# Issuing a kernel's side stream of weights from GpSimd's queue, and spacing its first part wider

## The chip, the cores and the metric

The kernel runs on one core of a Trainium2 chip. The metric is the device time of one execution in microseconds. Before the change three runs took 2155.38, 2155.86 and 2158.86 us, median 2155.86.

## The reference

One block of a network on 256 tokens of 2048 numbers, all in float32: a feed-forward layer, a mixer and a second feed-forward layer, each wrapped in the same way.

```python
def sandwich_sublayer(x, fn, gain_pre, gain_post, shift, scale, gate, weight):
    h = modulate(rms_norm(x, gain_pre), shift, scale)
...
def swiglu(h, w_gate, w_up, w_down):
    return (jax.nn.silu(h @ w_gate) * (h @ w_up)) @ w_down
...
    return jnp.concatenate([y_pool, y_rwkv], axis=-1) @ w_out
```

Each sublayer adds its gated, normalized result to `x`. The feed-forward layers have 5632 hidden numbers; the mixer projects with `w_in`, runs a pooling branch and a recurrence (24 heads of 64), and projects back with `w_out`. The nine vectors of the **modulation** (shift, scale and gate of three sublayers) are one product of a single row, `silu(c) @ w_ada + b_ada`, with a weight matrix of 2048 x 18432: 151 MB, used for nothing else. Vectors 0 to 2 belong to the first feed-forward layer (FFN1), 3 to 5 to the mixer, 6 to 8 to the second (FFN2).

## The kernel before

**Products.** Every weight tile is split in two parts for the sake of precision: ACT copies it to a rounded `hi` (L179), DVE subtracts to get `lo` (L180), and PE makes three products of each tile (`mm3` L189 to L191, `mm3_wide` L196 and L197, `rows_mm` L523 to L525). I call such a pair of hi and lo a piece. Pieces have four buffers, so DVE and ACT can be at most four pieces ahead of PE. The weights themselves come by `load` (L169), one DMA of up to 1 MB on SyncE's queue (SP), into four raw buffers in the FFNs and two in the mixer.

**The modulation** runs beside all this on DVE. `ada_begin` (L205) lists its work as 76 steps in the order of vectors (1,0), 2, 4, 3, 5, 7, 6, 8. The first 20 steps make vectors 1 and 0 together, ahead of FFN1's first products, with transfers of 256 KB (L238). Each later vector has eight steps, four for either half: a step (`ada_step`, L220) issues four transfers of 512 KB on SP (L235) into tiles named `ada` (four buffers in the FFNs, two in the mixer), and DVE multiplies each by its part of silu(c) and adds it to an accumulator, `acc` (L242 for the first, L244 for the others). After the last of a half vector DVE transposes the accumulator (L256), reduces it (L258), PE makes four small products (L261), and DVE adds the bias into `mod` (L264). These DVE instructions are given low priority (`later`), and a scheduler that works on the whole program sets the order in which they stand on DVE between the splits. Every engine then runs its own list in that order.

**When a step is begun.** The layers call `tick` at each chunk of weights, and every so many chunks it begins a step: `ADA_FFN1` = 2.8 in FFN1 (L616, 84 chunks tick), 3 in the mixer (42 chunks tick) and in its last product w_out (16), 12 in FFN2. At fixed places `ada_finish` (L267) begins all the steps that are still missing for a vector: vector 3 before FFN1's last product, vector 5 before w_out, vector 6 before w_out's last quarter (L847, `q == 3`), vector 8 before FFN2's last product. In FFN1 84 / 2.8 gives 30 steps: the 24 of vectors 2, 4 and 3, and six of vector 5.

**FFN1** goes through gate and up for the first hidden columns with all of the reduction (`outer`), its down product, then two more groups of gate, up and down. Its pieces are number 0 to 263 in DVE's order; those of the mixer 264 to 504, with w_out from 441 on, in the quarters q = 0 (two at once), 2 and 3; FFN2's follow.

**The last quarter of w_out** is written by `rows_block` with `apart`: it has three banks, `sb` (first 128 tokens), `y` and `mm` (two halves of the others), and the pieces of its last eight rows are held back, so that each bank is finished apart. `mm` stands in a pool of two banks that the modulation's small products (L261) share.

Of the kernel before, what the change touches and what calls it, by code (L numbers as in the profile page):

```python
# [18 lines left out]
D = 2048  # L19
# [8 lines left out]
TICKS = (1, 3, 7)  # L28
GROUPS1 = (20, 16, 8)
GROUPS2 = (12, 12, 12, 8)  # L30
ADA_FFN1, ADA_MIXER, ADA_OUT, ADA_FFN2 = 2.8, 3, 3, 12
BLOCKS = ((0, 2), (2, 2), (4, 4), (8, 4), (12, 4))
POOL_WIDTH = 512
POOL_WINDOWS = (2, 4, 8, 16)
# [42 lines left out]
class Block:  # L77
# [142 lines left out]
    def ada_step(self, psum):  # L220
        nc = self.nc
        if self.ada_pos == len(self.ada_tasks):
            return
        cols, k0 = self.ada_tasks[self.ada_pos]
        width = cols[0][2]
        (v0, c0, _), (v1, c1, _) = cols
        per = 512 // width
        if k0 == 0:
            self.acc = self.tile(self.accs, [P, 2, width], tag="acc")
        acc = self.acc  # L230
        for kk in range(k0, k0 + 4, per):
            raw = self.tile(self.raws, [P, per, 2, width], tag="ada", bufs=self.ada_bufs)
            w = self.I["w_ada"][kk * P:(kk + per) * P, :].rearrange("(k p) c -> p k c", p=P)
            if (v0, c0 + width) == (v1, c1):
                nc.sync.dma_start(raw.rearrange("p k j c -> p k (j c)"), w[:, :, v0 * D + c0:v0 * D + c0 + 2 * width])  # L235
            else:
                for j, (v, c, _) in enumerate(cols):
                    nc.sync.dma_start(raw[:, :, j, :], w[:, :, v * D + c:v * D + c + width])  # L238
            for i in range(per):
                ck = self.csilu[:, kk + i:kk + i + 1]  # L240
                if kk + i == 0:
                    self.later(nc.vector.tensor_scalar(acc, raw[:, i], ck, None, ALU.mult))  # L242
                else:
                    self.later(nc.vector.scalar_tensor_tensor(acc, raw[:, i], ck, acc, ALU.mult, ALU.add))  # L244
        self.ada_pos += 1
        if k0 == KD - 4:
            n = width // P
            ps = self.tile(psum, [P, 512], tag="mm")[:, :2 * n]
            if v0 != v1:
                for i in range(2 * n):  # L250
                    nc.tensor.matmul(ps[:, i:i + 1], acc[:, i // n, i % n * P:(i % n + 1) * P], self.ones[:, :1],
                                     start=True, stop=True)
            else:

                flip = self.tile(self.raws, [P, 2 * width], tag="ada", bufs=self.ada_bufs)
                nc.vector.transpose(flip, acc.rearrange("p j c -> p (j c)"))  # L256
                sums = self.tile(self.small, [P, 2 * n, 4], tag="sums")
                nc.vector.tensor_reduce(sums.rearrange("p k q -> p (k q)"), flip.rearrange("p (b t) -> p b t", t=32),  # L258
                                        mybir.AxisListType.X, ALU.add)
                for q in range(4):  # L260
                    nc.tensor.matmul(ps[32 * q:32 * q + 32, :], self.quads, sums[:, :, q], start=True, stop=True)  # L261
            for j, (v, c, _) in enumerate(cols):
                for a, m, ap in self.columns("b_ada", v * KD + c // P, n):
                    nc.vector.tensor_tensor(self.mod[:, v, c // P + a:c // P + a + m], ps[:, j * n + a:j * n + a + m],  # L264
                                            ap, ALU.add)
# [1000 lines left out]
```

## Time and profile before

| | |
|---|---|
| runs before the change | 2155.38, 2155.86, 2158.86 us |
| the profiled execution, its own time | 2157.36 us |
| its span in the profile | 2155.6 us |
| mean granted clock of TensorE | 0.984 |
| DMA packets | 502.31 MB, mean 233 GB/s |
| HBM read | 497.77 MB |

The span is what the profile covers of the execution; 1.8 us lie around it. The page gives the busy time of each engine, the span in slices, the chain of work that ended last, and groups of instructions by line: count, busy time, mean duration in ns, and the idle time just before them with what ended it. PE is TensorE's products, PEld its weight loads, DVE VectorE, ACT ScalarE, POOL GpSimd, SP SyncE, SPq SyncE's sequencer. Other views cut out a stretch of time (windows), list every wait by what ended it, or list instructions in order of time.

### The profile page before, as it was taken

To read this page: it belongs to the slowest core of one execution; us is meant where nothing else is said; L and a number is where in the kernel's file an instruction comes from. 1 tells how busy PE (TensorE), PEld (TensorE's weight loads), DVE (VectorE), ACT (ScalarE), POOL (GpSimd) and SP (SyncE) were. 2 spreads that over 40 slices of the span, in tenths; PEclk is the share of its full clock that TensorE was granted. 3 is DMA by queue.
4 is the path that set the end of the run, shared out by engine and by line. 5 is a ranking of instruction groups with operands and counts; after the bars stand their busy time and mean duration, and the time that the engine had idled before them with its cause. 6 is when DMAs were issued, how large, how long until landed. Compare 5 with 4: busy or idle time off the path is not lost.

```text
span 2155.6 us, 37182 instructions
## 1 busy us (share of the span) xinstructions
PE 2072.4 (96%) x14955; PEld 1802.4 (84%) x14955; DVE 1621.2 (75%) x2523; ACT 1079.1 (50%) x1823; POOL 0.2 (0%) x4
## 2 busy tenths in 40 slices
PE   4999999999999998899999999999999999999998
PEld 3999988888888877888887866799888888888887
DVE  6788898798877778899998877788755555555556
ACT  4534543444433455765656654665434444444453
POOL 0000000000000000000000000000000000000000
PEclk8999999999999999999999979999999999999999
DMA  9999888999888748845644526599755555555553
GB/s 317 359 315 322 289 282 306 323 336 315 304 308 294 277 141 243 258 140 173 192 137 147 182 81 195 169 311 320 254 195 194 180 193 196 187 185 195 194 181 133
DMA packets 316570, 502.31 MB, mean 233 GB/s; under 512 B 12037, under 2 KB 197486, under 8 KB 316142
## 3 DMA queue, kind: packets, MB, share of 16 engines
q1 hardware_dynamic: 314380, 496.32, 68.6%
q10 hardware_dynamic: 2018, 3.62, 0.5%
q8 instruction: 117, 1.92, 0.4%
q14 instruction: 55, 0.45, 0.1%
HBM read 497.77 MB, written 2.12 MB: 232 GB/s over the span
## 4 chain that ended last, share of the span: by engine, by line
PE 83%; DMA 7%; DVE 6%; ACT 3%; issue 2%; SPq 0%; DVEq 0%; ACTq 0%
PE mm L196 21%; PE mm L197 10%; PE mm L191 7%; PE mm L190 7%; PE mm L189 7%; PE mm L523 7%; PE mm L525 7%; PE mm L524 7%; DMA ada<-in_w_ada_dram 5%; DVE lo L180 2%; DVE acc L244 1%; DMA raw<-in_w_in_dram 1%; ACT hi L179 1%; PE sb L1110 1%; PE sb L1145 0%
## 5 line engine op out<-in xcount | busy, mean ns | idle before, releaser
L179 ACT CAST hi<-raw 128x1024 fp32r<-128x1024 f32 (+2 forms) x768 | 694.6, 911 | 780.7 <-PE mm L525 266.9
L180 DVE TENSOR_TENSOR lo<-raw,hi 128x1024 fp32r<-128x1024 f32 (+2 forms) x768 | 796.4, 1048 | 351.6 <-ACT hi L179 348.5
L196 PE MATMUL mm<-hT,hi 128*128 128x512 f32 x1984 | 698.6, 395 | 0.0
L197 PE MATMUL mm<-hT,lo 128*128 128x256 f32 x1984 | 558.3, 281 | 2.4 <-DVE lo L180 2.4
L196 PEld LDWEIGHTS mm<-hT,hi 128*128 128x128 f32 x1984 | 373.8, 188 | 87.9
L244 DVE SCALAR_TENSOR_TENSOR acc<-ada,csilu,acc 128x1024 f32<-128x1024 f32 (+1 forms) x285 | 349.0, 1225 | 96.7 <-DMA ada<-in_w_ada_dram 94.7
L190 PE MATMUL mm<-hT,hi 128*128 128x256 f32 x1376 | 395.0, 288 | 3.4 <-DVE hT L362 3.4
L189 PE MATMUL mm<-hT,hi 128*128 128x256 f32 x1376 | 392.0, 289 | 4.0 <-ACT hT L357 3.8
L191 PE MATMUL mm<-hT,lo 128*128 128x256 f32 x1376 | 393.2, 287 | 0.5 <-DVE lo L180 0.5
L197 PEld LDWEIGHTS mm<-hT,lo 128*128 128x128 f32 x1984 | 372.8, 188 | 3.3 <-DVE lo L180 3.1
L189 PEld LDWEIGHTS mm<-hT,hi 128*128 128x128 f32 x1376 | 260.9, 191 | 10.6 <-ACT hT L357 6.1
L190 PEld LDWEIGHTS mm<-hT,hi 128*128 128x128 f32 x1376 | 261.9, 190 | 9.1 <-DVE hT L362 5.5
L191 PEld LDWEIGHTS mm<-hT,lo 128*128 128x128 f32 x1376 | 261.9, 191 | 4.5 <-DVE lo L180 0.7
L523 PE MATMUL mm<-hi,act 128*128 128x512 f32 (+1 forms) x688 | 264.9, 385 | 0.0
L524 PE MATMUL mm<-lo,act 128*128 128x512 f32 (+1 forms) x688 | 264.5, 384 | 0.0
L525 PE MATMUL mm<-hi,act 128*128 128x512 f32 (+1 forms) x688 | 264.4, 384 | 0.0
L524 PEld LDWEIGHTS mm<-lo,act 128*128 128x128 f32 x688 | 129.3, 188 | 25.9 <-DVE lo L180 0.6
L525 PEld LDWEIGHTS mm<-hi,act 128*128 128x128 f32 x688 | 129.3, 188 | 25.7
L523 PEld LDWEIGHTS mm<-hi,act 128*128 128x128 f32 x688 | 129.3, 188 | 25.6
L641 ACT ACTIVATE silu<-silu 128x512 f32<-128x512 f32 x31 | 19.6, 632 | 58.0 <-DVE silu L640 58.0
L644 ACT CAST act<-silu 128x512 fp32r<-128x512 f32 x31 | 19.2, 618 | 31.1 <-DVE silu L642 31.1
L606 DVE TENSOR_TENSOR act<-act,mm 128x512 f32<-128x512 f32 x48 | 32.2, 681 | 1.8 <-PE mm L191 1.6
(371 smaller groups left out, 1936.2 us busy)
## 6 DMA issues: line engine op xcount, KB each, us to landing
ada<-in_w_ada_dram SPq DMA_DIRECT2D x224, 512.0 KB
raw<-in_ffn_w_down_dram SPq DMA_DIRECT2D x88, 1024.0 KB
raw<-in_ffn_w_gate_dram SPq DMA_DIRECT2D x84, 1024.0 KB
raw<-in_ffn_w_up_dram SPq DMA_DIRECT2D x84, 1024.0 KB
raw<-in_w_in_dram SPq DMA_DIRECT2D x34, 1024.0 KB
ada<-in_w_ada_dram SPq DMA_DIRECT2D x128, 256.0 KB
raw<-in_w_out_dram SPq DMA_DIRECT2D x16, 1024.0 KB
raw<-in_w_in_dram SPq DMA_DIRECT2D x9, 512.0 KB
```

Of the source, the lines that this page charges most:

```text
L179: a = nc.scalar.copy(hi, raw)
L180: d = nc.vector.tensor_tensor(lo, raw, hi.bitcast(F32), ALU.subtract)
L189: nc.tensor.matmul(ps, hi, x[:, 0, :], start=start, stop=False)
L190: nc.tensor.matmul(ps, hi, x[:, 1, :], start=False, stop=False)
L191: nc.tensor.matmul(ps, lo, x[:, 0, :], start=False, stop=stop)
L196: nc.tensor.matmul(ps.rearrange("p a t -> p (a t)"), hi, x.rearrange("p a t -> p (a t)"), start=start, stop=False)
L197: nc.tensor.matmul(ps[:, 0, :], lo, x[:, 0, :], start=False, stop=stop)
L244: self.later(nc.vector.scalar_tensor_tensor(acc, raw[:, i], ck, acc, ALU.mult, ALU.add))
L523: nc.tensor.matmul(ps, x[:, 0, ts], hi, start=start, stop=False)
L524: nc.tensor.matmul(ps, x[:, 0, ts], lo, start=False, stop=False)
L525: nc.tensor.matmul(ps, x[:, 1, ts], hi, start=False, stop=stop)
L606: nc.vector.tensor_tensor(part, part, bank, ALU.add)
```

## The change

Two edits. The transfers of all steps after the first 20, 224 DMAs of 512 KB, are issued by GpSimd's queue and no longer by SP's. And in FFN1 a step is begun every 3.5 chunks, which makes 84 / 3.5 = 24 steps: vectors 2, 4 and 3. The six steps of vector 5 (24 transfers, 24 additions on DVE) are begun in the mixer.

```diff
-ADA_FFN1, ADA_MIXER, ADA_OUT, ADA_FFN2 = 2.8, 3, 3, 12
+ADA_FFN1, ADA_MIXER, ADA_OUT, ADA_FFN2 = 3.5, 3, 3, 12
...
             raw = self.tile(self.raws, [P, per, 2, width], tag="ada", bufs=self.ada_bufs)
+
+            queue = nc.sync if self.ada_pos < self.ada_end[(1, 0)] else nc.gpsimd
             w = self.I["w_ada"][kk * P:(kk + per) * P, :].rearrange("(k p) c -> p k c", p=P)
             if (v0, c0 + width) == (v1, c1):
-                nc.sync.dma_start(raw.rearrange("p k j c -> p k (j c)"), w[:, :, v0 * D + c0:v0 * D + c0 + 2 * width])
+                queue.dma_start(raw.rearrange("p k j c -> p k (j c)"), w[:, :, v0 * D + c0:v0 * D + c0 + 2 * width])
             else:
                 for j, (v, c, _) in enumerate(cols):
-                    nc.sync.dma_start(raw[:, :, j, :], w[:, :, v * D + c:v * D + c + width])
+                    queue.dma_start(raw[:, :, j, :], w[:, :, v * D + c:v * D + c + width])
```

From here on lines of the changed kernel are two higher: L244 is L246, L256 and L258 are L258 and L260, L261 is L263, L523 to L525 are L525 to L527.

The scheduler orders the whole program anew. The first place is on DVE in FFN1's second group of gate and up, near piece 100. `acc<-ada` is an addition, `lo<-raw,hi` the split of a piece. Before:

```order
L180 TENSOR_TENSOR lo_3492<-raw_3473,hi_3491 128x1024
L180 TENSOR_TENSOR lo_3514<-raw_3511,hi_3513 128x1024
L244 SCALAR_TENSOR_TENSOR acc_3638<-ada_3766,csilu_95,acc_3638 128x1024
L180 TENSOR_TENSOR lo_3530<-raw_3511,hi_3529 128x1024
L180 TENSOR_TENSOR lo_3571<-raw_3545,hi_3570 128x1024
L703 COPY y_93<-mm_3311 128x512
L703 COPY y_93<-mm_3312 128x512
L244 SCALAR_TENSOR_TENSOR acc_3638<-ada_3871,csilu_95,acc_3638 128x1024
L180 TENSOR_TENSOR lo_3587<-raw_3545,hi_3586 128x1024
L180 TENSOR_TENSOR lo_3605<-raw_3602,hi_3604 128x1024
L244 SCALAR_TENSOR_TENSOR acc_3638<-ada_3874,csilu_95,acc_3638 128x1024
```

And now:

```order
L246 SCALAR_TENSOR_TENSOR acc_3778<-ada_4239,csilu_95,acc_3778 128x1024
L246 SCALAR_TENSOR_TENSOR acc_3778<-ada_4242,csilu_95,acc_3778 128x1024
L180 TENSOR_TENSOR lo_3514<-raw_3499,hi_3513 128x1024
L246 SCALAR_TENSOR_TENSOR acc_3778<-ada_4245,csilu_95,acc_3778 128x1024
L180 TENSOR_TENSOR lo_3530<-raw_3499,hi_3529 128x1024
L258 STREAM_TRANSPOSE ada_4249<-acc_3778 128x1024
L180 TENSOR_TENSOR lo_3548<-raw_3545,hi_3547 128x1024
L705 COPY y_93<-mm_3311 128x512
L705 COPY y_93<-mm_3312 128x512
L260 TENSOR_REDUCE sums_4251<-ada_4249 128x32
L180 TENSOR_TENSOR lo_3564<-raw_3545,hi_3563 128x1024
```

Four to five pieces stand in each; the additions stand closer, and a half vector ends there with its transpose and reduction. Counted over DVE's order from piece 80 to piece 168, 65 additions stood there before and 85 now; from piece 176 to the end of FFN1, where there were 45, there are none.

The second place is on DVE in the last quarter of w_out. The splits of its first rows write `lo`; `y`, `G`, `base` and `row` are the sums of the output rows. Before:

```order
L180 TENSOR_TENSOR lo_15630<-raw_15627,hi_15629 128x512
L180 TENSOR_TENSOR lo_15643<-raw_15627,hi_15642 128x512
L180 TENSOR_TENSOR lo_15656<-raw_15627,hi_15655 128x512
L412 TENSOR_TENSOR y_93<-pb_15391,G_14997 128x512
L180 TENSOR_TENSOR lo_15669<-raw_15627,hi_15668 128x512
L413 SCALAR_TENSOR_TENSOR G_14998,stats_15009<-x_92,y_93 128x512
L426 TENSOR_REDUCE base_15600<-stats_15009 128x3
L180 TENSOR_TENSOR lo_15684<-raw_15681,hi_15683 128x512
L493 TENSOR_SCALAR row_15602<-base_15600 128x1
L412 TENSOR_TENSOR y_93<-zb_15392,G_14997 128x512
L494 TENSOR_SCALAR row_15603<-row_15602 128x1
L493 TENSOR_SCALAR row_15606<-sxx_7520 128x1
```

And now, from the last two of four held-back pieces on, which are split ahead of their turn (`S` and `bk` are their places):

```order
L180 TENSOR_TENSOR S_2889_15746<-raw_15735,SV_15745 128x512
L180 TENSOR_TENSOR bk_15750<-raw_15735,ar_15749 128x512
L246 SCALAR_TENSOR_TENSOR acc_15567<-ada_15598,csilu_95,acc_15567 128x1024
L246 SCALAR_TENSOR_TENSOR acc_15567<-ada_15601,csilu_95,acc_15567 128x1024
L246 SCALAR_TENSOR_TENSOR acc_15567<-ada_15604,csilu_95,acc_15567 128x1024
L246 SCALAR_TENSOR_TENSOR acc_15567<-ada_15607,csilu_95,acc_15567 128x1024
L246 SCALAR_TENSOR_TENSOR acc_15567<-ada_15610,csilu_95,acc_15567 128x1024
L246 SCALAR_TENSOR_TENSOR acc_15567<-ada_15613,csilu_95,acc_15567 128x1024
L258 STREAM_TRANSPOSE ada_15617<-acc_15567 128x1024
L260 TENSOR_REDUCE sums_15619<-ada_15617 128x32
L266 TENSOR_TENSOR mod_105<-mm_15616,cols_29_130 128x4 x2
L180 TENSOR_TENSOR lo_15684<-raw_15681,hi_15683 128x512
```

No addition stood there before. Now six follow each other, with the transpose, the reduction and the additions of the bias, which wait for PE's small products, and the split of the fifth piece (`hi_15683`) stands behind all of them; two more additions stand a little earlier.

The third place is PE's order in the same quarter, at the fourth piece. Before, each piece's products went into `sb`, `y` and `mm` one after the other:

```order
L523 MATMUL sb_15624<-hi_15629,hT_94 128x512
L524 MATMUL sb_15624<-lo_15630,hT_94 128x512
L525 MATMUL sb_15624<-hi_15629,hT_94 128x512
L523 MATMUL y_15625<-hi_15629,hT_94 128x256
L524 MATMUL y_15625<-lo_15630,hT_94 128x256
L525 MATMUL y_15625<-hi_15629,hT_94 128x256
L523 MATMUL mm_15626<-hi_15629,hT_94 128x256
L524 MATMUL mm_15626<-lo_15630,hT_94 128x256
L525 MATMUL mm_15626<-hi_15629,hT_94 128x256
L523 MATMUL sb_15624<-hi_15642,hT_94 128x512
```

And now:

```order
L525 MATMUL sb_15529<-hi_15668,hT_94 128x512
L526 MATMUL sb_15529<-lo_15669,hT_94 128x512
L527 MATMUL sb_15529<-hi_15668,hT_94 128x512
L525 MATMUL y_15530<-hi_15668,hT_94 128x256
L526 MATMUL y_15530<-lo_15669,hT_94 128x256
L527 MATMUL y_15530<-hi_15668,hT_94 128x256
L263 MATMUL mm_15616<-sums_15619,consts_69 32x8 x4
L525 MATMUL mm_15531<-hi_15629,hT_94 128x256
L526 MATMUL mm_15531<-lo_15630,hT_94 128x256
L527 MATMUL mm_15531<-hi_15629,hT_94 128x256
```

The first four pieces go into `sb` and `y` alone; the small products of vector 6's second half stand next (`mm<-sums`), and the products of those four pieces into `mm` only behind them.

## The prediction

> **What bounds the kernel now.** I read the page first: its busy shares, its chain, and the groups of the modulation's instructions.
>
> ```profile
> PE 2072.4 (96%) x14955; PEld 1802.4 (84%) x14955; DVE 1621.2 (75%) x2523; ACT 1079.1 (50%) x1823; POOL 0.2 (0%) x4
> PE 83%; DMA 7%; DVE 6%; ACT 3%; issue 2%; SPq 0%; DVEq 0%; ACTq 0%
> L244 DVE SCALAR_TENSOR_TENSOR acc<-ada,csilu,acc 128x1024 f32<-128x1024 f32 (+1 forms) x285 | 349.0, 1225 | 96.7 <-DMA ada<-in_w_ada_dram 94.7
> L256 DVE STREAM_TRANSPOSE ada<-acc 128x1024 f32<-128x1024 f32 x14 | 17.4, 1240 | 0.2
> L258 DVE TENSOR_REDUCE sums<-ada 128x32 f32<-128x1024 f32 x14 | 16.9, 1210 | 0.1
> ada<-in_w_ada_dram SPq DMA_DIRECT2D x224, 512.0 KB
> ```
>
> PE is busy for 96% of the span, so only PE's idle time, or its slow time, can be won; anything that stops PE is paid in full. The modulation's additions (I call one such DVE instruction an addition) wait 94.7 us for their weights. Whether that costs anything is read stage by stage, in the windows (us of PE, PEld, DVE, ACT and POOL, then granted clock, DMA share, GB/s): FFN1 to 700, the mixer's start to 925, its recurrence to 1300, w_out to 1400, FFN2's start to 1480.
>
> ```profile
> 277.00:523.00 246.00, 246.00 (x1296) 209.85 (x1295) 209.11 (x218) 108.35 (x127) 0.00 (x0) 1.00 0.90 314
> 523.00:675.00 152.00, 151.99 (x770) 127.48 (x769) 124.83 (x126) 63.97 (x72) 0.00 (x0) 1.00 0.89 313
> 675.00:700.00 25.00, 22.55 (x121) 19.39 (x120) 17.92 (x20) 9.61 (x14) 0.00 (x0) 0.93 0.71 250
> 807.00:925.00 118.00, 100.70 (x861) 92.68 (x860) 99.33 (x189) 75.42 (x158) 0.00 (x0) 0.99 0.78 240
> 925.00:1300.00 375.00, 361.88 (x4755) 304.39 (x4753) 330.86 (x892) 227.82 (x615) 0.00 (x0) 0.96 0.49 151
> 1300.00:1400.00 100.00, 98.70 (x504) 75.74 (x502) 69.27 (x148) 54.48 (x126) 0.00 (x0) 0.97 0.56 181
> 1400.00:1480.00 80.00, 74.44 (x603) 72.38 (x603) 67.64 (x82) 50.92 (x76) 0.00 (x0) 0.98 0.91 314
> ```
>
> In FFN1 from 277 to 675 PE never stands still, though DMA is nine tenths occupied and DVE waits: those waits are covered by the four split pieces that DVE may be ahead. FFN1 loses time at one place only, 675 to 700; the waits there and the chain show how.
>
> ```profile
> PE mm L197 <- DVE lo L180: 2.4, 1, 2.4
> 682.02 9.06 DMA ada<-in_w_ada_dram
> 691.18 1.28 DVE acc L244
> 692.71 1.23 DVE lo L180
> 694.00:698.00 4.00, 4.00 (x14) 3.43 (x15) 4.00 (x5) 0.77 (x2) 0.00 (x0) 0.57 0.06 18
> ```
>
> The chain waits 9.06 us for one ada transfer, the addition and the next split follow on DVE, and PE stands for 2.4 us; in the 4 us after that stop PE's granted clock is 0.57. So this change can win at most a few us in FFN1. The mixer from 807 and FFN2's start have idle PE (17.3, 13.1 and 5.6 us), and the end of w_out almost none.
>
> **The change part by part.** *The issuing queue.* The bytes are the same; only who issues them changes. On SP a weight load stands behind an ada transfer that waits for its buffer, and the reverse:
>
> ```profile
> SPq L169 <- DVE lo L180: 1031.5, 229, 11.3
> SPq L235 <- DVE acc L244: 113.0, 42, 19.7
> ```
>
> The second row's 113.0 us of blocking goes, since GpSimd's queue holds nothing else (POOL x4 on the page). But the first row is nine times longer: loads mostly wait for their own buffer. The stall at 691 is of the kind that goes, as no addition is left in that stage: its 2.4 us, and 43% of 4 us at clock 0.57, **-4**. By the Trainium skill's page "DMA: Bandwidth & Descriptors", section "Issuing engines are not separate DMA queues", transfers of all issuers interleave on the same 16 engines, and only the sequencer's time is saved; by it the queue alone brings no rate, the -4 stands, and the faster rival below loses most of what it counts on; no run here shows this yet.
>
> *FFN1's additions.* Six steps (24 transfers of 512 KB, 24 additions) leave FFN1, but the order packs the remaining ones: from split 80 to 168 of DVE's order stood 65 additions, now 85, and after 176 none. That stretch is the window 277 to 523.
>
> ```profile
> L180 DVE TENSOR_TENSOR lo<-raw,hi 128x1024 fp32r<-128x1024 f32 x89 | 107.0, 1218 | 5.7 <-ACT hi L179 5.3
> L244 DVE SCALAR_TENSOR_TENSOR acc<-ada,csilu,acc 128x1024 f32<-128x1024 f32 x57 | 73.0, 1281 | 26.9 <-DMA ada<-in_w_ada_dram 26.6
> ```
>
> DVE: 209.1 + 20 x 1.28 + two more transposes and reductions (4.9) = 239.6 of 246 us, 97%. DMA: 314 GB/s x 246 us = 77.2 MB (80.2 by 88 pieces and 65 additions of 0.524 MB each); with 10.5 more, 87.7 to 90.7 MB. At 314/0.90 = 349 GB/s that takes 251 to 260 us, 5 to 14 over the window. Four weight buffers ahead are a stock of 4.2 MB, 12 us. So between nothing and 12; I take **+3**, nearer to none, since the stock covers most.
>
> *The end of w_out.* Here the six steps come back. Before, the ticks reached the end of vector 6; now its last steps are emitted ahead of the last quarter (`ada_finish`), and PE's order puts the four products of that sum (L261 of before, L263 now) between the second and the third part of the first four row pieces. PE cannot pass them. They need six additions in a row, a transpose and a reduction, which DVE has ahead of its next split. What PE did there before, and after the line of dots DVE (start, us, engine, line):
>
> ```profile
> 1372.96 0.39 PE L523 MATMUL sb<-hi,hT 128*128 128x512 f32 x1
> 1373.65 0.28 PE L523 MATMUL y<-hi,hT 128*128 128x256 f32 x1
> 1374.01 0.28 PE L523 MATMUL mm<-hi,hT 128*128 128x256 f32 x1
> 1374.36 0.39 PE L523 MATMUL sb<-hi,hT 128*128 128x512 f32 x1
> ...
> 1373.81 0.69 DVE L180 TENSOR_TENSOR lo<-raw,hi 128x512 fp32r<-128x512 f32 x1
> 1374.42 0.68 DVE L413 SCALAR_TENSOR_TENSOR G<-x,y 128x512 f32<-128x512 f32 x1
> 1375.99 0.68 DVE L412 TENSOR_TENSOR y<-zb,G 128x512 f32<-128x512 f32 x1
> ```
>
> One piece takes PE 1374.36 - 1372.96 = 1.40 us, of which sb and y 1.05; four of these and PE is at L263 at 1372.96 + 4.2 = 1377.2. DVE is through the fourth piece's split at 1374.4; then come about 3 us of the row sums (four such rows at the spacing of 0.61 that 1373.81 and 1374.42 show, and small ones), two additions at 1.22 and four splits at 0.61 (4.9), six additions (7.3), transpose and reduction (2.4): 1392.0. Without one wait for data PE stands 14.8 us. But the mixer has two ada buffers, so the last eight additions go in rounds of two: free, transfer, add. Two waits of the chain, in this kernel's mixer, show what a transfer takes once its buffer is free:
>
> ```profile
> 869.87 4.70 DMA ada<-in_w_ada_dram
> 999.70 7.51 DMA ada<-in_w_ada_dram
> ```
>
> With 4.70: the eighth last addition ends near 1377.9, three rounds of 4.70 + 1.22 follow, to 1395.7, the partner ends 1.8 later, transpose and reduction 2.4: 1399.9, so **22.7** of standing. With 7.51 it is 31. I take 4.70, the shorter, since PE stands and little else is moved. By the Trainium skill's page "DMA: Bandwidth & Descriptors", section "Anatomy of one DMA — SWDGE (gpsimd) path", such a transfer takes about 2.0 us plus its bytes at 436 GB/s, 3.2 us here (an estimate); by it the standing is 4.5 us shorter and the sum 2178.5. The next split and its product cost **+1** more. Then the clock:
>
> ```profile
> 1272.00:1291.00 19.00, 18.69 (x230) 12.07 (x228) 11.81 (x42) 6.88 (x24) 0.00 (x0) 0.50 0.14 44
> ```
>
> After a stop of 2.4 us it was 0.57 for 4 us (1.7 lost); here it was half for 19 us. I take **+2**, as the first row's stop is the only one of DVE's making (1.7 to 9.5, half of 19).
>
> *Mixer.* Until 1300 it has about five additions more (6.4 us of DVE, which is at 331 of 375 there), and the mixed queue's waits may go:
>
> ```profile
> ACT hi L179 <- DMA raw<-in_w_in_dram: 13.5, 9, 3.9
> DVE acc L244 <- DMA ada<-in_w_ada_dram: 5.5, 3, 3.0
> ```
>
> From -15 (both rows and part of the clock) to +6; I take **-2**, because the chain there is mostly the recurrence's own.
>
> *FFN2's start.* The first four ada transfers were issued on SP behind the first four weight loads:
>
> ```profile
> 1396.36 0.47 SPq L169 DMA_DIRECT2D raw<-in_ffn_w_up_dram  x1
> 1396.87 1.59 SPq L235 DMA_DIRECT2D ada<-in_w_ada_dram  x3
> ```
>
> Now they go beside them: 2.1 MB at 349 GB/s is 6.0 us, half of it ahead of the first weights: **+3** (0 to 10, with three more additions in the first thirty splits).
>
> Sum: -4 + 3 + 22.7 + 1 + 2 - 2 + 3 = +25.7. The profiled execution took 2157.36 (its span of 2155.6 and 1.8 around it): 2183. It stands 1.5 above the median of the runs, 2155.86, so **2181**.
>
> **The rivals.**
> - *The burst is fed in time and the queue pays* (faster). If GpSimd's queue lets the additions ahead of the burst run early, so that PE stands at L263 for less than about 10 us, and the mixer's waits (13.5 and 5.5), FFN1's 4 and FFN2's 5.6 all go, the sum is 10 - 28.6 = -18.6: 2137. For it: these waits are of two queues mixed in one. Against it: the order itself, with 14.8 us of DVE work ahead of PE. It decides from a DVE that is over 5 us ahead of PE at split 492. 0.12.
> - *Even.* The floor of 14.8 and the mixer's lower bound of -15 nearly cancel, and the small terms with them: 2152 to 2160. 0.06.
> - *FFN1 starves* (slower still). DVE at 97% has no room for waits: if additions wait the same 26.6 us as before, DVE needs 266 of 246 us and PE stands for 20 in place of the 3 above: 2181 + 17 = 2198, and up to 2208 with the clock after each stop. For it: DMA at 0.90 already. 0.10.
> - *GpSimd cannot write its transfers while DVE works* (slower; the queue does not do what is meant). Each transfer would start an addition's length, 1.28 us, later; three rounds in the burst add 4, and FFN1's 26.6 us of waits, a quarter longer, add some 7: about 2192. The copying form that could hold it up is rare:
>
> ```profile
> L242 DVE TENSOR_SCALAR acc<-ada,csilu 128x1024 f32<-128x1024 f32 (+1 forms) x19 | 13.7, 721 | 6.6 <-DMA ada<-in_w_ada_dram 6.6
> ```
>
> The Trainium skill's page "SBUF — State Buffer", the box on the "DVE blocks DMA" trap in section "SBUF: two separate sides", states such a hold-up for DVE's two-port copies with GpSimd-issued transfers; no run here shows it yet. 0.04.
>
> **How the numbers follow.** 0.68 for the forecast, 0.14 for the slower rivals: slower 0.82; even 0.06; faster 0.12 (0.2%, 4.3 us, is about what a measurement of this kernel can tell from no change). The range: below, the forecast with the floor of 14.8 (-8) and the mixer's whole gain (-13) is 2160, and the even case is taken in from 2154; above, transfers of 7.51 (+8), FFN1 at its bound (+9) and most of the clock's (+6) are 2204. That leaves out the faster rival and part of those above. The likeliest case alone has 2165 to 2200.
>
> **What would show it.** Right: in the last quarter of w_out one wait of PE, 15 to 30 us at L263, for the reduction, with DVE waiting for ada in between and a lower clock behind it; no stop at 691; PE without a stop in FFN1; DVE near 97% between 277 and 523. Wrong: PE going through that place, additions of vector 6 done long before it, or PE waiting for splits between 277 and 523 for over 10 us.

## The result and the profile after

The changed kernel takes 2213.84 us (median of four runs, 2208.39 to 2216.79) against 2157.36 of the kernel before (four runs, 2155.38 to 2163.72): slower, ratio 1.0254, 95% interval 1.0224 to 1.0284. That is +56 us where +25 was forecast, outside the range on record. The profiled execution is the fastest of the four, 2208.39, 51.0 above that of before.

The page of the changed kernel first: busy shares, chain, the additions, and the transfers on their new queue.

```profile
PE 2080.5 (94%) x14955; PEld 1805.6 (82%) x14955; DVE 1618.3 (73%) x2523; ACT 1080.1 (49%) x1823; POOL 118.6 (5%) x228
PE 78%; DMA 8%; DVE 7%; issue 4%; ACT 3%; POOL 0%; SPq 0%; DVEq 0%; POOLq 0%; ACTq 0%
L246 DVE SCALAR_TENSOR_TENSOR acc<-ada,csilu,acc 128x1024 f32<-128x1024 f32 (+1 forms) x285 | 348.6, 1223 | 59.5 <-DMA ada<-in_w_ada_dram 56.8
ada<-in_w_ada_dram POOLq DMA_DIRECT2D x224, 512.0 KB, 6.2
```

The additions wait 57 us for their weights in place of 95, and the kernel is slower: the sum of that wait says nothing of the time. The stages do (windows, same columns as before):

```profile
277.00:523.00 246.00, 246.00 (x1294) 209.73 (x1293) 236.77 (x243) 106.08 (x125) 42.78 (x81) 1.00 1.00 360
523.00:675.00 152.00, 152.00 (x766) 128.14 (x765) 82.33 (x87) 65.92 (x75) 0.00 (x0) 1.00 0.59 194
675.00:700.00 25.00, 25.00 (x143) 21.79 (x142) 13.64 (x15) 11.64 (x16) 0.00 (x0) 1.00 0.61 202
807.00:925.00 118.00, 96.26 (x727) 88.67 (x726) 89.01 (x164) 69.41 (x142) 13.20 (x25) 0.93 0.77 235
1290.00:1397.00 107.00, 97.32 (x481) 72.20 (x476) 79.97 (x146) 46.79 (x106) 11.09 (x21) 0.86 0.66 221
1397.00:1423.00 26.00, 0.00 (x0) 0.00 (x0) 15.62 (x22) 2.38 (x6) 3.16 (x6) 0.58 0.61 205
1423.00:1437.00 14.00, 13.75 (x74) 12.24 (x75) 5.80 (x11) 4.95 (x8) 0.00 (x0) 0.80 0.00 0
```

FFN1 went as worked out: DVE 236.8 of 246 us, PE without a stop. The mixer's start has less of PE than before (96.3 for 100.7 in 118 us, clock 0.93), w_out's first quarters lost a tenth of theirs, and from 1397 to 1423 PE does nothing. The waits around that stop, then POOL's issues and DVE in it:

```profile
PE mm L263 <- DVE sums L260: 26.9, 1, 26.9
DVE acc L246 <- DMA ada<-in_w_ada_dram: 8.8, 4, 5.0
```

```profile
1405.69 0.53 POOL L237 DMA_DIRECT2D ada<-in_w_ada_dram  x1 [4.73 <-DMA ada<-in_w_ada_dram]
1407.15 0.53 POOL L237 DMA_DIRECT2D ada<-in_w_ada_dram  x1 [0.94 <-DVE acc L246]
1413.45 0.53 POOL L237 DMA_DIRECT2D ada<-in_w_ada_dram  x1 [5.77 <-DVE acc L246]
```

```profile
1404.12 1.28 DVE L246 SCALAR_TENSOR_TENSOR acc<-ada,csilu,acc 128x1024 f32<-128x1024 f32 x1
1405.57 1.28 DVE L246 SCALAR_TENSOR_TENSOR acc<-ada,csilu,acc 128x1024 f32<-128x1024 f32 x1 [0.18 <-DMA ada<-in_w_ada_dram]
1411.87 2.60 DVE L246 SCALAR_TENSOR_TENSOR acc<-ada,csilu,acc 128x1024 f32<-128x1024 f32 x2 [5.01 <-DMA ada<-in_w_ada_dram]
1417.58 1.28 DVE L246 SCALAR_TENSOR_TENSOR acc<-ada,csilu,acc 128x1024 f32<-128x1024 f32 x1 [3.11 <-DMA ada<-in_w_ada_dram]
1419.38 1.28 DVE L246 SCALAR_TENSOR_TENSOR acc<-ada,csilu,acc 128x1024 f32<-128x1024 f32 x1 [0.51 <-DMA ada<-in_w_ada_dram]
```

The rounds of two are plain: an addition ends at 1405.4, its buffer's transfer is issued at 1405.7 and used at 1411.9, and so on until the reduction.

Where the 51 us arose is seen by setting the starts of PE's products side by side. Both executions have 14955 in nearly the same order; the row gives the start of the n-th in either trace.

| n, place | before, us | after, us | behind by | gained in the stretch | forecast for it |
|---|---|---|---|---|---|
| 4750, mixer begins | 815.0 | 809.0 | -5.9 | -5.9 | -4 + 3 |
| 10250, ahead of w_out | 1283.1 | 1293.8 | 10.7 | +16.6 | -2 |
| 10675, ahead of the stop | 1374.8 | 1395.4 | 20.6 | +9.9 | none |
| 10750, behind the stop | 1387.3 | 1436.1 | 48.7 | +28.1 | 22.7 + 1 + 2 |
| 11750, FFN2 under way | 1537.9 | 1588.6 | 50.7 | +2.0 | +3 |

So the sizes set for the stop, its clock and FFN2's start were nearly met. The mixer and the first quarters of w_out, 26.5 us together, were put at -2.

### The profile page after: what moved, and what is told of

It is laid out like the page before. It is cut to its first block, busy times and chain, and to the rows that moved or that the text cites. A ratio compares the mean times of both kernels' runs of the same rounds, so it can differ in the third digit from the quotient of the medians.

```text
span 2206.6 us, 37398 instructions
## 1 busy us (share of the span) xinstructions
PE 2080.5 (94%) x14955; PEld 1805.6 (82%) x14955; DVE 1618.3 (73%) x2523; ACT 1080.1 (49%) x1823; POOL 118.6 (5%) x228
## 3 DMA queue, kind: packets, MB, share of 16 engines
q0 software_dynamic: 32256, 117.45, 15.3%
## 4 chain that ended last, share of the span: by engine, by line
PE 78%; DMA 8%; DVE 7%; issue 4%; ACT 3%; POOL 0%; SPq 0%; DVEq 0%; POOLq 0%; ACTq 0%
PE mm L196 21%; PE mm L197 11%; PE mm L525 7%; PE mm L526 7%; PE mm L527 7%; PE mm L190 6%; PE mm L191 6%; PE mm L189 6%; DMA ada<-in_w_ada_dram 4%; DMA raw<-in_w_in_dram 2%; DVE lo L180 2%; DVE acc L246 1%; ACT hi L179 1%; PE sb L1112 1%; PE sb L1106 0%
## 5 line engine op out<-in xcount | busy, mean ns | idle before, releaser
L246 DVE SCALAR_TENSOR_TENSOR acc<-ada,csilu,acc 128x1024 f32<-128x1024 f32 (+1 forms) x285 | 348.6, 1223 | 59.5 <-DMA ada<-in_w_ada_dram 56.8
L525 PE MATMUL mm<-hi,act 128*128 128x512 f32 (+1 forms) x688 | 264.8, 385 | 0.0
L527 PE MATMUL mm<-hi,act 128*128 128x512 f32 (+1 forms) x688 | 264.3, 384 | 0.0
L237 POOL DMA_DIRECT2D ada<-in_w_ada_dram x224 | 118.4, 529 | 1420.8 <-DVE acc L246 630.6
L527 PEld LDWEIGHTS mm<-hi,act 128*128 128x128 f32 x688 | 129.3, 188 | 25.7
L525 PEld LDWEIGHTS mm<-hi,act 128*128 128x128 f32 x688 | 129.3, 188 | 25.7
```

The costliest lines, as they stand in the source:

```text
L237: queue.dma_start(raw.rearrange("p k j c -> p k (j c)"), w[:, :, v0 * D + c0:v0 * D + c0 + 2 * width])
L525: nc.tensor.matmul(ps, x[:, 0, ts], hi, start=start, stop=False)
L527: nc.tensor.matmul(ps, x[:, 1, ts], hi, start=False, stop=stop)
```

## The experiments

All eighteen are told. Each was measured against the kernel before on the same chip (medians there 2156 to 2158 us).

### The two halves of the change

The first two kernels have one edit of the change each; the next two let GpSimd issue in one stage alone. The values and the choice of queue:

```diff
 a28, after:   ADA_FFN1 = 3.5 -> 2.8
 b35, before:  ADA_FFN1 = 2.8 -> 3.5
 q1only, a28:  queue = nc.gpsimd if self.ada_end[(1, 0)] <= self.ada_pos < self.ada_end[(1, 0)] + 30 * 1 else nc.sync
 qmix, a28:    queue = nc.gpsimd if 50 <= self.ada_pos < 68 else nc.sync
```

> The queue alone: GpSimd issues the 224 transfers, a step is begun every 2.8 chunks in FFN1 as before. Theory 1 (two separate costs: the spacing makes the stop at the end of w_out, 28 us, the queue makes the mixer slower, about 17 us from 815 to 900 and 1 later, and saves 6 in FFN1): no stop in w_out's last quarter, the mixer's start still behind, +10 to +18 us against the kernel before, about 2170. Theory 2 (the six added steps make the mixer slower too, the queue only saves): 6 us faster, about 2151. Theory 3 (the queue alone makes nearly everything, the stop too): +45 or more.

> The spacing alone: 3.5 chunks, all transfers on SyncE's queue. Theory 1: the stop of PE at the small products in the last quarter of w_out is there (25 to 30 us), the mixer's start is as before, w_out's first part may lose a few us: +25 to +35 us, about 2187. Theory 2: +45 to +55, about 2207. Theory 3: within 5 us of the kernel before.

> GpSimd issues only the 30 steps that FFN1 begins (2.8 chunks), SyncE's queue those of the mixer and FFN2. Theory 1: FFN1's gain alone, no stop near 691, the mixer as before: 2 to 6 us faster than the kernel before. Theory 2: the same gain, 6. Theory 3, or a queue of GpSimd that is dear anywhere: 0 or slower.

> GpSimd issues only the 18 steps of the mixer (2.8 chunks in FFN1), SyncE's queue the others. Theory 1: the stop near 691 stays, the mixer's start is 10 to 17 us behind: +10 to +20 us. Theory 2: the mixer as before, within 4 us of the kernel before.

| kernel | median, us | ratio to before (95%) |
|---|---|---|
| a28, the queue alone | 2174.01 | 1.0087 (1.0057 to 1.0116) |
| b35, the spacing alone | 2206.55 | 1.0236 (1.0220 to 1.0252) |
| q1only, GpSimd in FFN1 | 2157.17 | 1.0010 (0.9996 to 1.0023) |
| qmix, GpSimd in the mixer | 2178.72 | 1.0114 (1.0092 to 1.0137) |

The spacing alone costs nearly all, 50 us, more than theory 1 had; the queue alone 19, and all of that in the mixer. In FFN1 the queue is worth nothing at 2.8 chunks: the stop at 691 is missing in qmix too, whose FFN1 stands as before (PE 3.00 of 3 us there), so it belonged to that one execution and was never the change's to win. By the starts of the products, as in the table above and in one execution of each, the mixer (product 4750 to 10250) loses 11.2 us in a28 and 2.4 in b35, the front of w_out (10250 to 10675) 1.6 and 6.9: the changed kernel's +16.6 there is mostly the queue's, its +9.9 mostly the spacing's. The two costs do not add up (50 + 19 for 56), because the stop is longer in b35, where DVE's order leaves twelve additions for it instead of six:

```profile
PE mm L263 <- DVE sums L260: 41.8, 1, 41.8
DVE acc L246 <- DMA ada<-in_w_ada_dram: 16.7, 10, 4.9
```

### The queue's cost in the mixer: order or transfers

In qmix DVE's order has the mixer's additions earlier: by the kernel's own order 70 of them stand ahead of the first piece of w_out, 63 before, and the later ones up to 22 pieces sooner. The next two kernels part that order from the queue. A table gives the last 60 of the mixer's 72 additions a piece each (the numbers are read from the order of the other kernel), and a dependency that asks for nothing but order holds it there: in qpin the addition behind that piece, as shown, in spin the next piece behind the addition.

```diff
 qpin = qmix, spin = before, both with
+        self.splits.append(d)
+        for op in self.pending.pop(len(self.splits) - 1, ()):
+            self.after(op, d, "pin")
...
-                    self.later(nc.vector.scalar_tensor_tensor(acc, raw[:, i], ck, acc, ALU.mult, ALU.add))
+                    self.pin(nc.vector.scalar_tensor_tensor(acc, raw[:, i], ck, acc, ALU.mult, ALU.add))
```

> GpSimd issues the mixer's 72 transfers as in qmix, but each of the mixer's additions is pinned on DVE behind the piece that stands ahead of it in the kernel before, so that DVE's order is nearly that of before (qmix had them up to 20 pieces earlier). If the order makes the mixer's cost: within 5 us of the kernel before, about 2159. If the transfers of GpSimd's queue make it (they land later, or take the engines from the weights): +15 to +25 us as qmix had it, about 2177.

> All transfers on SyncE's queue and 2.8 chunks, as before, but the pieces of the mixer are pinned behind the additions that stand ahead of them in qmix, so that DVE's order is qmix's. If the order makes the mixer's cost: +15 to +25 us, about 2177. If the transfers make it: within 5 us of the kernel before.

qpin (GpSimd's transfers, the order of before, some additions up to nine pieces later): 2164.10 us, ratio 1.0032 (1.0014 to 1.0051). spin (SyncE's transfers, qmix's order to within three pieces): 2177.11, ratio 1.0088 (1.0070 to 1.0107). So of qmix's 1.14% the order makes about 0.9 and the transfers 0.3, and the two add up. The windows of qmix and then qpin over the recurrence show it on PE:

```profile
925.00:1300.00 375.00, 354.39 (x4749) 298.12 (x4749) 324.87 (x878) 224.81 (x608) 24.80 (x47) 0.97 0.52 158
```

```profile
925.00:1300.00 375.00, 361.83 (x4792) 305.73 (x4791) 324.35 (x884) 228.03 (x617) 21.33 (x41) 0.96 0.49 148
```

DVE's busy time is the same, 324.9 and 324.4; with the additions earlier PE gets 7.4 us less. Cut at the same products, from the 4750th to the 10250th, the kernel before, qmix and spin show two ways of paying:

```profile
815.00:1283.10 468.10, 442.44 (x5504) 382.51 (x5502) 411.70 (x1039) 292.68 (x749) 0.00 (x0) 0.97 0.57 176
810.50:1297.30 486.80, 448.76 (x5503) 385.43 (x5501) 415.52 (x1040) 293.31 (x749) 36.94 (x70) 0.97 0.58 176
810.60:1310.30 499.70, 466.24 (x5503) 400.44 (x5501) 416.72 (x1035) 291.55 (x749) 0.00 (x0) 0.92 0.56 172
```

qmix needs 18.7 us more than before; PE's idle time grows by 12.4 (25.7 to 38.0), and the granted clock is the same. spin needs 31.6 more; its idle time grows by 7.8 only, and the clock falls to 0.92. So in one execution the earlier order is paid mostly in waits, in the other mostly in clock. What in the order does it (an addition ahead of a step of the recurrence, or one that stands on DVE before its weights have landed) was not taken apart further.

### The moved steps: one place or spread

If the stop were the loss, an order without it would save it. m22 and ms22 begin steps more often in the mixer and in w_out, so that the ticks finish vector 6 and `ada_finish` finds nothing left.

```diff
 m22 = after, ms22 = b35, both with
-ADA_FFN1, ADA_MIXER, ADA_OUT, ADA_FFN2 = 3.5, 3, 3, 12
+ADA_FFN1, ADA_MIXER, ADA_OUT, ADA_FFN2 = 3.5, 2.2, 2.5, 12
```

> The changed kernel, but steps are begun every 2.2 chunks in the mixer and every 2.5 in w_out, so that vector 6 is done by the ticks and no addition is left for w_out's last quarter. If the stop there costs what PE stands (27 us, and a little clock): 28 us less than the changed kernel, about 2185, with no stop at L263. If the additions cost the same wherever they are put: within 10 us of the changed kernel, about 2208.

> The same ticks (3.5 in FFN1, 2.2 in the mixer, 2.5 in w_out) with all transfers on SyncE's queue. If the stop of 42 us makes nearly all that the spacing alone costs: 40 to 45 us less than b35, about 2163, and 15 to 25 below m22. If the additions cost the same wherever they are put: about 2200.

m22 takes 2208.30 us (ratio 1.0221, 1.0194 to 1.0247), ms22 2201.43 (1.0205, 1.0182 to 1.0228). Neither has a stop over 5 us from the mixer on, and each is only 5 to 7 us below the kernel with its stop. The theory that the stop is the cost fell here: by the same count of products ms22 falls 45 us behind between the mixer's start and product 10675, where b35 had fallen 9 behind ahead of its stop. The steps cost nearly the same, paid in small waits and a lower clock, as the windows between these two products show for the kernel before and ms22:

```profile
815.00:1374.80 559.80, 529.59 (x5927) 446.78 (x5926) 474.87 (x1153) 338.23 (x850) 0.00 (x0) 0.96 0.57 176
809.40:1413.90 604.50, 555.64 (x5927) 459.26 (x5926) 499.11 (x1177) 335.18 (x844) 0.00 (x0) 0.92 0.59 183
```

PE's idle time grows from 30.2 to 48.9 us. The rest, some 26 us, is about what the fall of the clock makes (an estimate: 8% of 604.5 against 4% of 559.8).

### What a moved step is made of

x24 keeps b35's transfers and makes 23 of the additions narrow (their columns are left out of the product); t24 keeps the additions whole and cuts those steps' transfers from 24 to 6 (each step uses its first tile four times, so that part of the product is another one); x22 is x24's edit where the steps are spread.

```diff
 x24 = b35, x22 = ms22, both with
+                    n = 8 if 62 <= self.ada_pos < 68 else width
-                    self.later(nc.vector.scalar_tensor_tensor(acc, raw[:, i], ck, acc, ALU.mult, ALU.add))
+                    self.later(nc.vector.scalar_tensor_tensor(acc[:, :, :n], raw[:, i, :, :n], ck, acc[:, :, :n], ALU.mult, ALU.add))
 t24 = b35 with the transfer and its tile under
+            if kk == k0 or not 62 <= self.ada_pos < 68:
```

> The spacing alone as in b35, but 23 additions of the last six steps of vector 6 take only 16 columns of each tile in place of 1024 (this part of the product is left out); the transfers, buffers, transposes and reductions stay. If DVE's work of the moved additions makes the cost: 20 to 30 us less than b35, about 2180, and the stop of 42 us at most 25. If their transfers in rounds of two buffers make it: within 10 us of b35, about 2200, the stop still 35 or more.

> b35 with the transfers of the last six steps of vector 6 cut from 24 to 6: each step's four additions read its first tile (that part of the product is left out); all additions are whole. If rounds of two transfers set the stop: a stop of 10 to 20 us in place of 42 and 25 to 35 us less than b35, about 2177. If DVE's additions set it: 35 us or more of stop, within 10 us of b35.

> ms22 (the six steps spread over the mixer and w_out) with the additions of the last six steps cut to 16 columns, transfers kept (part of the product is left out). If the additions' DVE time is the price of spread steps: 20 to 30 us less than ms22, about 2177. If it is the wait for transfers through two buffers: within 10 us of ms22, about 2195.

| kernel | median, us | ratio to before (95%) | the stop, us |
|---|---|---|---|
| b35 | 2206.55 | 1.0236 (1.0220 to 1.0252) | 41.8 |
| x24, additions narrow | 2197.91 | 1.0172 (1.0145 to 1.0199) | 36.1 |
| t24, transfers cut | 2180.32 | 1.0101 (1.0073 to 1.0129) | 17.5 |
| ms22, spread | 2201.43 | 1.0205 (1.0182 to 1.0228) | none |
| x22, spread, narrow | 2192.28 | 1.0150 (1.0115 to 1.0185) | none |

The stops are read from one execution of each; that of x24 is the slowest of its five, 2209.12. Taking away some 24 us of DVE's work saves 9 by the medians and 14 by the ratios; taking away 18 transfers saves 26 and 29. In the stop the transfers through two buffers are the larger part (t24's order also leaves six additions for it, not twelve). Of the spread steps only x22 speaks, and only for w_out: the 23 narrow additions are 23 of the 24 that stand in w_out's first quarters, and all of the mixer's 72 are whole. By the starts of the products, in one execution of each, the front of w_out loses 15.3 us in ms22 and 5.3 in x22, so there DVE's time is the larger part, unlike in the stop. The mixer loses 29.4 and 26.8; what makes that no run took apart. The stop in b35, x24 and t24, DVE's additions and what ended the idle time ahead of each:

```profile
1401.67 1.28 DVE L246 SCALAR_TENSOR_TENSOR acc<-ada,csilu,acc 128x1024 f32<-128x1024 f32 x1 [2.55 <-DMA ada<-in_w_ada_dram]
1403.81 1.28 DVE L246 SCALAR_TENSOR_TENSOR acc<-ada,csilu,acc 128x1024 f32<-128x1024 f32 x1 [0.86 <-DMA ada<-in_w_ada_dram]
1406.76 1.28 DVE L246 SCALAR_TENSOR_TENSOR acc<-ada,csilu,acc 128x1024 f32<-128x1024 f32 x1 [1.66 <-DMA ada<-in_w_ada_dram]
...
1411.94 1.29 DVE L246 SCALAR_TENSOR_TENSOR acc<-ada,csilu,acc 128x1024 f32<-128x1024 f32 x1 [1.51 <-DMA ada<-in_w_ada_dram]
```

```profile
1407.25 0.23 DVE L247 SCALAR_TENSOR_TENSOR acc<-ada,csilu,acc 128x16 f32<-128x16 f32 x1 [1.02 <-DMA ada<-in_w_ada_dram]
1409.83 0.23 DVE L247 SCALAR_TENSOR_TENSOR acc<-ada,csilu,acc 128x16 f32<-128x16 f32 x1 [2.35 <-DMA ada<-in_w_ada_dram]
1412.25 0.23 DVE L247 SCALAR_TENSOR_TENSOR acc<-ada,csilu,acc 128x16 f32<-128x16 f32 x1 [2.18 <-DMA ada<-in_w_ada_dram]
```

```profile
1396.58 5.25 DVE L247 SCALAR_TENSOR_TENSOR acc<-ada,csilu,acc 128x1024 f32<-128x1024 f32 x4
```

A round of two takes 5.1 to 5.3 us in b35 (1401.67 to 1406.76, 1406.76 to 1411.94) and still 4.4 to 5.0 with narrow additions (1407.25 to 1412.25 is the longest), the time a buffer needs to be filled and emptied; without transfers four additions take 5.25. So an addition that waits in a row through two buffers is priced at about 2.6 us, not at 1.22. A third ada buffer in the mixer was not tried.

### How the price grows, and how much room FFN1 has

Steps moved half as far, and then the other way, out of the mixer into FFN1, with either queue there.

```diff
 b31, b24 (from before):       ADA_FFN1 = 2.8 -> 3.1, 2.4
 q24, q22, q20, q175 (q1only): ADA_FFN1 = 2.8 -> 2.4, 2.2, 2.0, 1.75, GpSimd for all the steps begun in FFN1
 a24 (from after):             ADA_FFN1 = 3.5 -> 2.4
```

> SyncE's queue alone, a step every 3.1 chunks in FFN1: three steps (12 additions) move to the mixer in place of six, and vector 6 is done by the ticks before the last quarter. If each addition that moves costs about 2 us wherever it lands: half of b35, +22 to +28 us, about 2182. If only the stop in the last quarter costs: within 8 us of the kernel before.

> SyncE's queue alone, a step every 2.4 chunks in FFN1: five steps (20 additions) move the other way, from the mixer into FFN1. If additions are free in FFN1 and cost about 2 us each from the mixer on: 20 to 40 us faster than the kernel before, about 2125. If FFN1 is full (its DMA share is 0.90 up to 675): PE stops in FFN1 and what the mixer gains is given back there, within 8 us of the kernel before or slower.

> The same 2.4 chunks with GpSimd's queue for the 35 steps that FFN1 begins, SyncE's for the others. If additions are free in FFN1: 20 to 40 us faster than the kernel before, as b24; the queue in FFN1 is worth nothing more, within 5 us of b24. If the room in FFN1 is what counts, the denser order of GpSimd's queue, which leaves more room to FFN1's end, makes it faster than b24 by 5 or more.

> The changed kernel with 2.4 chunks in place of 3.5: GpSimd's queue everywhere, five steps more in FFN1 than the kernel before. If the earlier order in the mixer costs wherever GpSimd's queue issues there: 15 to 25 us slower than q24, about 2165. If that cost came with the mixer's load alone: within 5 us of q24, about 2146.

> q24 with 2.2 chunks: 38 steps in FFN1, eight more than before, three more than q24, GpSimd's queue in FFN1 alone. If FFN1 still has room: 5 to 10 us less than q24, about 2138. If FFN1 is full: PE stops there, and the time is q24's or more, 2146 to 2160.

> q22 with 2.0 chunks: 42 steps in FFN1, six left for the mixer, GpSimd's queue in FFN1 alone. If FFN1 still hides additions and transfers: about 1.2 us for each of the 16 additions that leave the mixer, 2120 or less. If FFN1 is full (q22 moved 368 GB/s there): PE stops in FFN1, 2136 or more.

> The same with 1.75 chunks: all 48 steps of vectors 2, 4, 3, 5, 7 and 6 in FFN1, none in the mixer. If FFN1 still hides them: 2105 or less. If FFN1 is full: PE waits for splits in its last part for more than the mixer gains, 2136 or more.

| kernel | steps in FFN1 | queue in FFN1, mixer | median, us | ratio to before (95%) |
|---|---|---|---|---|
| b35 | 24 | SP, SP | 2206.55 | 1.0236 (1.0220 to 1.0252) |
| b31 | 27 | SP, SP | 2171.71 | 1.0064 (1.0044 to 1.0085) |
| b24 | 35 | SP, SP | 2155.76 | 0.9996 (0.9974 to 1.0017) |
| q24 | 35 | POOL, SP | 2145.71 | 0.9944 (0.9922 to 0.9965) |
| a24 | 35 | POOL, POOL | 2157.05 | 0.9998 (0.9981 to 1.0014) |
| q22 | 38 | POOL, SP | 2135.76 | 0.9899 (0.9876 to 0.9922) |
| q20 | 42 | POOL, SP | 2129.08 | 0.9871 (0.9853 to 0.9889) |
| q175 | 48 | POOL, SP | 2144.95 | 0.9941 (0.9921 to 0.9960) |

The price is no constant. Each kernel against before on its own chip, sixteen additions in the mixer cost 5 us from q20 to q22, 0.3 each; from before to b31 twelve cost 14, 1.2 each; from b31 to b35, where the stop appears, the next twelve cost 36, 3 each. b31's expectation of half b35's loss was a miss for that reason; q20 came between its two, and b24's gain of 20 to 40 us did not come. a24 against q24 shows that GpSimd's queue in the mixer and FFN2 still costs 11 us when the mixer holds fewer steps.

FFN1, which the prediction had taken to be nearly full, had room for eighteen steps more than the changed kernel gives it. With SP's queue the room ends earlier: b24 has a stop of PE in FFN1 that q24 has not, and takes 10 us more. Whether the queue or its order makes that is not shown: of the additions in FFN1 60 stand behind piece 176 in b24 and 35 in q24, 26 and none behind piece 220, and no run held the order. q175 (35 behind piece 220) is past the end on GpSimd's queue too; q20 (18 there) is not. The waits of b24 (690 to 725) and of q175 (523 to 830), each for a half vector's reduction:

```profile
PE mm L263 <- DVE sums L260: 8.1, 1, 8.1
```

```profile
PE mm L263 <- DVE sums L260: 15.6, 4, 8.0
```

And FFN1 and the recurrence of q20, the fastest kernel:

```profile
277.00:523.00 246.00, 246.00 (x1314) 209.74 (x1313) 240.29 (x251) 108.21 (x125) 44.85 (x85) 1.00 1.02 367
523.00:675.00 152.00, 152.00 (x771) 128.01 (x770) 148.80 (x150) 64.42 (x71) 29.57 (x56) 1.00 1.03 375
925.00:1300.00 375.00, 371.81 (x4835) 310.58 (x4825) 297.13 (x864) 239.46 (x648) 0.00 (x0) 1.00 0.34 100
```

DVE is at 98% from 277 to 675 and PE does not stand still once; the recurrence has PE at 99% with a full clock, where the kernel before had 361.9 of 375 at 0.96. q20 beats both kernels: GpSimd's queue, or the order that comes with it, helps in FFN1 alone and with the spacing moved the other way.

## Why the prediction was wrong

- **Direction and the stop: right.** PE stands at L263 for the reduction, in rounds of two buffers, 26.9 us where 22.7 were worked out; the two rounds took 6.3 (1405.57 to 1411.87) and 5.7 us (1411.87 to 1417.58) where 4.70 + 1.22 had been set. The stretch with the stop, its restart and its clock grew by 28.1, forecast 25.7. The clock behind it, 0.80 for 14 us, lost 2.8; +2 was forecast.
- **The mixer: the step that failed.** It was put at -2, "because the chain there is mostly the recurrence's own", with about five additions more at 1.28 (four came). It took +16.6, and the front of w_out, for which there was no term, +9.9. Two things were missed. The new queue moves the mixer's additions forward in DVE's order, which alone costs 19 us (spin) and with the transfers' own 7 (qpin) makes qmix's 25: the orders were compared at the end of w_out and in FFN1, but not here. And eleven moved additions stand in w_out's first quarters; the spacing alone loses 6.9 us there (b35). In the stop an addition pays for its turn through two buffers (x24, t24), in w_out's front rather for DVE's time, as far as x22 shows. Why an addition that stands earlier costs PE so much in the mixer stays open.
- **FFN1: taken too dear, and its gain was chance.** The stretch had 61 additions before by the trace (57 at L244 and 4 at L242 in its window), not 65, so 24 came to it and not 20; DVE came to 236.8 us, below the 239.6 worked out. The denser additions cost nothing that can be told (q1only, 1.0010), as the four raw buffers cover them; the lower end of 0 to 12 held. The -4 for the stop at 691 was no effect of the queue, since qmix lacks the stop with FFN1 unchanged; one execution's stop of 2.4 us should not have been a term. That the mixer began 5.9 us early, near -4 of the forecast, is chance too: it begins 3.5 to 4.4 early in b35, q1only and qmix, whatever issues FFN1's transfers.
- **FFN2's start: the size near, the cause not borne out.** It took +2.0 for +3; but the same stretch takes +0.3 in a28, where GpSimd issues too, and +1.7 in qmix, where SP does.
- **The rivals.** The faster one fell, and the even one with it: the mixer's waits were not won. FFN1 did not starve. GpSimd's issues show no hold-up: the 224 take 527 to 662 ns, median 527, in the changed kernel. The rule of the Trainium skill on the "DVE blocks DMA" trap ("SBUF — State Buffer", "SBUF: two separate sides") is not seen here, where few DVE instructions are of the copying kind. The rule of the Trainium skill's page "DMA: Bandwidth & Descriptors", "Issuing engines are not separate DMA queues", held for q1only. q24 is 10 us faster than b24 with FFN1 loaded; as DVE's order differs too, that does not speak against it.
- **Range.** Its upper end added slower transfers in the stop, FFN1 and the clock. The mixer's own upper bound of +6 was not in it, and was 10 us too low: it was worked out from DVE's time, while order and transfers made the cost.
- **Slips of the working, without effect on the outcome.** The mixer's lower bound of -15 was said to hold both rows, but these make 19.0 (13.5 + 5.5). The 2178.5 by the page on transfers is counted from the profiled execution; from the median, as the forecast is, it is 2177.

## What to carry to other kernels

A side stream of work is free only where the stage that hosts it has slack in all that it uses: before moving it, find where its engine's wait ends last, and where its instructions wait in a row count the rounds of their buffers, not only their own time. When an edit changes a queue, compare the scheduler's order in every stage that the queue serves, the tight ones first; here the order made three quarters of the queue's cost in the mixer. And a single stop of one execution is no term of a sum until a second execution has it.

## What was not expected of the hardware

FFN1 moves up to 375 GB/s with the DMA share at 1.03, where 349 had been taken as full from 314 at 0.90. With the side stream on a queue of its own, a weight load in FFN1 (277 to 523) needs nearly twice as long from its issue: a median of 4.8 us before and 8.5 in q1only, worked out by adding up the bytes of SP's packets in the order of their ends and setting them against the loads' sizes. The time did not show it (q1only, 1.0010); the loads have four buffers. In the mixer, worked out in the same way, an ada transfer on SP took a median of 3.5 us (925 to 1290, before) and on GpSimd's queue 4.2 in qmix by its own completion; that this makes the 7 us of qpin is not shown.
